# Projections inside the attention's plan, for a hybrid decoder step on one Trainium2 core

## The chip, the cores and the metric

The kernel runs on one core of one Trainium2 chip. The metric is the device time of one execution in microseconds (us); all inputs lie in the device's memory at the start, and the outputs lie there at the end. The names of the engines are those of the profile: PE is TensorE's matrix multiply, PEld its weight load, DVE the vector engine, ACT the scalar engine, POOL GpSimd, and SP the engine that issues nearly all transfers.

## The reference

One inference step of a decoder with two layers, for 256 tokens of a new prompt and 8 decoding sequences with 4 new tokens each (288 tokens in all, width 1024), in float32. Each layer is wrapped by two half-step SwiGLU networks (width 2816). Layer 0 mixes by a short gated convolution, layer 1 by a sparse attention with three branches. The change is in layer 1, whose core is:

```python
q, kv_c, kv_s, kv_w, gates = nsa_project(h, w_in)     # 1024 -> 1024 + 6 * 256 + 48
k_c, v_c = compress(kv_c, ...)                        # one key and value per 32 positions, through gelu
s_c = einsum(q, k_c) * scale ; p_c = softmax(s_c)     # compressed branch
imp = p_c summed over the 4 heads of a group, by blocks of 64
idx = top_k(imp with the first, the current and the previous block forced, 16)
o_s = softmax attention over the 16 chosen blocks     # selected branch
o_w = softmax attention over the last 512 positions   # window branch
o = gates[0] * o_c + gates[1] * o_s + gates[2] * o_w ; y = o @ w_out
```

There are 16 query heads of 64 and 4 key heads. The decoding sequences have 2048 past positions each, in pages of 128 rows that a page table names. The prompt has 8 compressed blocks and 4 selectable ones, so it selects all it may see. The projected keys and values are outputs too.

## The kernel before, in words

All activations stand transposed, features on the 128 partitions and the 288 tokens along the free dimension. A product of float32 numbers is made of three: weights and activations are split into a high and a low part (`whi`, `wlo`, `xh`, `xl`), and hi·hi, hi·lo and lo·hi add up in one bank of PSUM. One output tile of 128 features is thus 8 x 3 = 24 matmuls over 288 columns. `Weights` (from line 171) loads weights in chunks of 1 MB into a ring `raw` of four buffers on SP's queue, and splits them on ACT (`whi`, L238) and DVE (`wlo`, L247) into a ring `split` of four pairs.

The first 800 us hold layer 0 and the first network of layer 1, with the compression of the cached pages spread through them as fill. The function `nsa` (from L828) then has two parts.

- **Projections** (L1032 to L1111), in the order in which they are written: six pairs of tiles for the three kinds of keys and values, one tile of 48 gates, eight tiles of queries `qT`. A helper `later(n, f)` places the small work n ticks behind: the prompt's compression (`cmp_prompt_in`, `cmp_prompt`, 2, 3), the turning of values (`values_in`), the gates (through ACT's sigmoid), and, behind each query tile, that tile's compressed scores (`prompt_cmp`, L1094: the 128 query columns are the stationary operand, 16 compressed keys stream).
- **Attention**, whose order is made by a planner (`Plan`, L127). Each step has an engine, a time that it takes (`TAKES`), what it comes after, buffers that it holds, and a rank. The planner goes through the steps that could start earliest on an engine, within a tolerance `NEAR`, and takes the one of lowest rank; so it writes out an order for each engine, and waits are fitted to it. Ranks are tables of numbers: `HEADS`, `CHUNKS`, `TAILS` for the four pairs of sequences, `UNITS` for the prompt's eight head groups.

For a pair of sequences, a *head* (`small`, `max`, `parts`, `share`, `rank`, `best`) scores the compressed keys and the new tokens, and makes the mask of blocks. Five *chunks* follow (the window and four quarters of the past), each of two pages of 1 MB: scores (`S`, four stationary operands of 32 columns side by side), DVE's masked maximum (`top`), ACT's exponential, four transposes (`turn`), a copy on ACT, and the values (`V`, 16 matmuls). A *tail* weights and sums the five parts, and turns the result into `xh` and `xl` for the output projection (`out` is the matmul with `Sel`). A prompt unit has two sets of scores, eight exponentials, twelve transposes and a value step `p_v`. POOL scales the prompt's exponentials.

TensorE's array is used in several forms, by how many rows and columns the operands take: 128x128 for products and transposes, 128x32 for sequences' scores and values, 128x64 for the prompt's values and compression, 64x128 for the prompt's scores, and a few small ones.

Pages come from `load_pages` (L1012): into four buffers `early`, free `raw` buffers, and, once the products are over, the four `split` pairs. A buffer is refilled after the `V` step that read it. All pages and the weights of the output projection go through SP's one queue, in order. `attention_out` (L1513) multiplies by `w_nsa_out`; its first two tiles go part by part, all hi·hi first. Then the last network and the final norm follow; in the last network, POOL issues eight copies of 1 MB of the window cache from memory to memory (L1554).

Of the kernel before, what the change touches and what calls it, by code (L numbers as in the profile page):

```python
# [50 lines left out]
RINGS = dict(mm=4, tr=2, acc=2, U=2, PA=1, PB=1, S=3, PTs=2, small=2, pc=1, score=1, mk=2, sum=2, PTm=2)  # L51
TAKES = dict(
    small=0.35, max=0.55, parts=0.9, share=0.35, rank=0.25, best=1.2, S=0.9, S2=1.0, top=0.62, top_w=0.8, exp=0.71, turn=0.5, copy=0.49,
    copy_v=0.61, V=1.0, og=0.16, min=0.2, wg=0.38, wg2=1.57, turn_s=0.18, copy_s=0.2, sum=1.36, V_s=0.35, add=0.2, last=0.33,
    own=0.21, out=0.25, oh_s=0.12, ol_s=0.13, cmp=1.38, cmp_e=0.3, cmp_n=1.93, cmp_t=0.33, cmp_c=0.4, s0=1.03, s1=0.65, t0=0.34,
    t1=0.215, e0=0.49, e1=0.385, factor=0.39, f0=1.92, f1=1.0, pturn=0.5, p_v=2.07, oh=0.28, ol=0.34, whi=0.96, wlo=2.4, wlo_v=1.15)
HOP = dict(PE=0.25, ACT=0.16, DVE=0.16, POOL=0.16, DMA=0.1)
LOAD, LAND, LOADED = 2.87, 1.5, 9.6


NEAR = 0.1
CHUNKS = (-56.4, -23.7, -3.8, -22.6, -17.9, 7.3, 5.5, -0.2, 6.9, 9.1, 15.5, 25.2, 19.4, 7.9, 21.5, 16.8, 30.3, 30.7, 32.2, 15.5)
HEADS, TAILS = (-33.5, -10.4, 15.4, 28.6), (-2.5, 14.2, 7.0, -34.2)
UNITS = (-2.6, 4.5, 6.9, 12.9, 16.9, 29.9, 36.5, 29.1)
COMPRESSED = -7.9
# [5 lines left out]
def weight_chunks():  # L71
# [24 lines left out]
    for t in range(6):  # L96
        yield "w_nsa_in", 0, steps[:KD], [range(D + t * 256, D + (t + 1) * 256)]
    yield "w_nsa_in", 0, steps[:KD], [range(D + 6 * 256, N_IN)]
    for pr in range(2):
        for gp in range(2):  # L100
            yield "w_nsa_in", 0, steps[:KD], [range((2 * pr + kp) * 256 + gp * P, (2 * pr + kp) * 256 + (gp + 1) * P) for kp in range(2)]

# [7 lines left out]
class Task:  # L110


    def __init__(self, engine, takes, put, after=(), slots=(), uses=(), rank=0.0):
        self.engine, self.takes, self.put, self.after, self.slots, self.rank = engine, takes, put, after, slots, rank
        self.end = None
        for x in (*slots, *uses):
            x.users.append(self)
# [9 lines left out]
class Plan:  # L127
# [3 lines left out]
    def __init__(self, rings):  # L131
        self.rings = {n: [None] * k for n, k in rings.items()}
        self.free, self.tasks = {}, []
# [6 lines left out]
    def start(self, t):  # L140

        at = self.free.get(t.engine, 0.0)
# [129 lines left out]
def tile_step(ctx, tc, x_turned, vectors, state_turned, cmp_pages, sel_pages, cache_win, win_pages, page_table,  # L272
# [555 lines left out]
    def nsa(at):  # L828
# [260 lines left out]
        def prompt_cmp(u):  # L1089
            if not u:  # L1090
                units["cs"] = accb()
# [522 lines left out]
```

## Time and profile before

| what | us |
|---|---|
| median of 3 runs | 1248.0 (1247.29 to 1249.34) |
| the profiled execution, its own time | 1246.98 |
| its span in the profile | 1245.2 |
| first projection matmul of the attention layer | 811.88 |
| first scores of a chunk of pages | 889.96 |
| first matmul of the output projection | 995.97 |

Times within the profile count from the start of the span. A row of the timeline has its start, its length up to the end of its last instruction, the engine, the line, the operation, and what it writes and reads; matmuls overlap, so a row's length exceeds the distance to the next row's start, and that distance is what a group costs.

### The profile page before, as it was taken

To read this page: it belongs to the slowest core of one execution; us is meant where nothing else is said; L and a number is where in the kernel's file an instruction comes from. 1 tells how busy PE (TensorE), PEld (TensorE's weight loads), DVE (VectorE), ACT (ScalarE), POOL (GpSimd) and SP (SyncE) were. 2 spreads that over 40 slices of the span, in tenths; PEclk is the share of its full clock that TensorE was granted. 3 is DMA by queue.
4 is the path that set the end of the run, shared out by engine and by line. 5 is a ranking of instruction groups with operands and counts; after the bars stand their busy time and mean duration, and the time that the engine had idled before them with its cause. 6 is when DMAs were issued, how large, how long until landed. Compare 5 with 4: busy or idle time off the path is not lost.

```text
span 1245.2 us, 25757 instructions
## 1 busy us (share of the span) xinstructions
PE 1227.8 (99%) x10047; PEld 1162.6 (93%) x10047; DVE 726.3 (58%) x1363; ACT 571.2 (46%) x1011; POOL 241.2 (19%) x237
## 2 busy tenths in 40 slices
PE   9999999999999999999999999999999999999997
PEld 8999999999999999999899999999866699999997
DVE  6663555666765545556564455677568566654554
ACT  6443344533544334335343344544377655433444
POOL 0260121221322201212120012130022222200211
PEclk9999999999999999999999999999999999999999
DMA  7764655756566466546563453496699857565422
GB/s 278 257 216 173 236 171 185 254 186 218 189 213 211 155 206 233 198 151 232 197 237 117 176 174 115 165 339 219 232 362 331 291 209 302 191 249 203 165 101 78
DMA packets 89066, 262.00 MB, mean 210 GB/s; under 512 B 9937, under 2 KB 43090, under 8 KB 73714
## 3 DMA queue, kind: packets, MB, share of 16 engines
q1 hardware_dynamic: 87922, 249.66, 57.0%
q0 software_dynamic: 256, 8.32, 1.7%
q10 hardware_dynamic: 768, 2.38, 0.5%
q8 instruction: 79, 1.29, 0.4%
q14 instruction: 41, 0.34, 0.1%
HBM read 257.31 MB, written 11.35 MB: 216 GB/s over the span
## 4 chain that ended last, share of the span: by engine, by line
PE 91%; DVE 3%; ACT 3%; DMA 2%; issue 1%; SPq 0%; POOL 0%; DVEq 0%; ACTq 0%
PE mm L303 82%; PE tr L303 5%; PE acc L303 3%; PE tr L334 1%; DMA early<-in_sel_pages_dram 1%; DVE wlo L247 1%; ACT S L1211 1%; DMA raw<-in_w_nsa_out_dram 0%; SPq L1008 0%; ACT L534 0%; ACT whi L238 0%; DMA wlo<-in_sel_pages_dram 0%; DMA raw<-in_w_ffa_gu_dram 0%; DVE xT L583 0%; ACT S L1367 0%
## 5 line engine op out<-in xcount | busy, mean ns | idle before, releaser
L303 PE MATMUL mm<-xh,whi 128*128 128x288 f32 x1832 | 543.3, 298 | 3.0 <-DVE xl L1476 1.1
L303 PE MATMUL mm<-xh,wlo 128*128 128x288 f32 x1832 | 539.9, 297 | 0.0
L303 PE MATMUL mm<-xl,whi 128*128 128x288 f32 x1832 | 532.8, 293 | 0.0
L247 DVE TENSOR_TENSOR wlo<-raw,whi 128x1024 fp32r<-128x1024 f32 (+2 forms) x361 | 407.8, 1143 | 94.3 <-ACT whi L238 91.5
L238 ACT ACTIVATE whi<-raw 128x1024 fp32r<-128x1024 f32 (+2 forms) x365 | 343.3, 952 | 100.3 <-PE mm L303 92.9
L303 PEld LDWEIGHTS mm<-xh,whi 128*128 128x128 f32 x1832 | 342.9, 188 | 8.8 <-issue 4.2
L303 PEld LDWEIGHTS mm<-xl,whi 128*128 128x128 f32 x1832 | 346.8, 190 | 0.3
L303 PEld LDWEIGHTS mm<-xh,wlo 128*128 128x128 f32 x1832 | 341.8, 187 | 0.6 <-DVE wlo L247 0.4
L303 PE MATMUL mm<-Ah,wlo 128*128 128x288 f32 x768 | 228.6, 298 | 1.0 <-DVE wlo L247 0.9
L303 PE MATMUL mm<-Ah,whi 128*128 128x288 f32 x768 | 227.9, 297 | 0.0
L303 PE MATMUL mm<-Al,whi 128*128 128x288 f32 x768 | 227.2, 296 | 0.0
L549 POOL TENSOR_TENSOR a<-s,t 128x288 f32<-128x288 f32 x80 | 110.3, 1379 | 517.8 <-DVE t L547 405.5
L303 PEld LDWEIGHTS mm<-Ah,wlo 128*128 128x128 f32 x768 | 144.2, 188 | 2.3 <-DVE wlo L247 2.1
L303 PEld LDWEIGHTS mm<-Ah,whi 128*128 128x128 f32 x768 | 145.0, 189 | 0.6 <-issue 0.4
L303 PEld LDWEIGHTS mm<-Al,whi 128*128 128x128 f32 x768 | 144.6, 188 | 0.0
L552 ACT ACTIVATE Ah<-a 128x288 fp32r<-128x288 f32 x88 | 39.1, 445 | 163.4 <-POOL a L549 150.1
L545 ACT ACTIVATE s<-t 128x288 f32<-128x288 f32 x88 | 39.1, 445 | 156.4 <-DVE t L543 156.3
L547 DVE TENSOR_TENSOR t<-mm,rB 128x288 f32<-128x288 f32 x88 | 40.2, 457 | 115.1 <-PE mm L303 115.1
L583 DVE SCALAR_TENSOR_TENSOR xT<-mm,xT 128x288 f32<-128x288 f32 x64 | 29.2, 456 | 90.1 <-PE mm L303 89.9
L553 DVE TENSOR_TENSOR Al<-a,Ah 128x288 fp32r<-128x288 f32 x88 | 40.8, 463 | 65.9 <-ACT Ah L552 65.9
L303 PE MATMUL tr<-cp,W 128*64 128x256 f32 x512 | 58.8, 382 | 0.0
L387 ACT ACTIVATE xh<-xT,vecT 128x288 fp32r<-128x288 f32 x48 | 25.2, 534 | 62.0 <-DVE xT L583 41.1
(283 smaller groups left out, 847.1 us busy)
## 6 DMA issues: line engine op xcount, KB each, us to landing
raw<-in_w_ffb_gu_dram SPq DMA_DIRECT2D x44, 1024.0 KB, 5.2
raw<-in_w_ffa_gu_dram SPq DMA_DIRECT2D x42, 1024.0 KB, 5.3
cp<-in_cmp_pages_dram SPq DMA_DIRECT2D x256, 128.0 KB, 4.3
early<-in_sel_pages_dram SPq DMA_DIRECT2D x56, 256.0 KB, 5.8
raw<-in_w_ffa_down_dram SPq DMA_DIRECT2D x16, 768.0 KB, 4.5
raw<-in_w_conv_in_dram SPq DMA_DIRECT2D x12, 1024.0 KB, 5.1
raw<-in_w_ffb_down_dram SPq DMA_DIRECT2D x16, 768.0 KB, 5.9
raw<-in_sel_pages_dram SPq DMA_DIRECT2D x48, 256.0 KB, 5.0
```

The costliest lines, as they stand in the source:

```text
L238: self.nc.scalar.activation(parts[0], v, AF.Copy)
L247: (lower or self.nc.vector).tensor_sub(parts[1], v, parts[0])
L303: nc.tensor.matmul(out, lhsT, rhs, start=start, stop=stop, skip_group_check=True)
L334: nc.tensor.transpose(out, in_, ident[:k, :k])
L387: nc.scalar.activation(normed[0][:, d], xT[:, d], AF.Copy, scale=vecT[:, v + d:v + d + 1])
L545: nc.scalar.activation(s1, t1, AF.Silu)
L547: nc.vector.tensor_mul(t2, pu[:, :N], rB)
L549: (nc.vector if last else nc.gpsimd).tensor_mul(a, s1, t2)
L552: nc.scalar.activation(Ah[:, f], a, AF.Copy)
L553: nc.vector.tensor_sub(Al[:, f], a, Ah[:, f])
L583: nc.vector.scalar_tensor_tensor(xT[:, d], py[:, :N], 0.5, xT[:, d], op0=OP.mult, op1=OP.add)
L1211: nc.scalar.activation(o, o, AF.Exp, scale=-1.0, bias=x, accum_out=e)
```

## The change

The queries are projected first, in the written order. Everything else that was projected in the written order, that is thirteen tiles (six pairs and the gates, in the order `SIDES`), becomes steps of the planner (`prod`, with splits `whi` and `wlo_v` and evictions `ev`), and so do the prompt's compression, the turning of values and the gates. So heads and chunks of the sequences, whose compressed keys are there already, may stand between products.

The planner also knows the form of the array: `MODES` gives one to each step of PE, a step in another form than the last one starts `SWITCH` = 0.12 later, and its rank counts `STAY` = 3.71 more. All times and ranks are new, with one rank for a step's first part and another for its second.

The compressed scores of the prompt are one step after the projections: `KcBD`, widened to 32 columns, is now the stationary operand and the queries stream (eight matmuls of 256 columns, four side by side), and a copy on ACT and four transposes bring them into the shape that the rest expects. The sigmoid and the tanh are worked out from ACT's exponential and DVE. The heads leave the scores of the new tokens to a step of their own. The fifth chunk's values are copied out of PSUM like the other four. During the projections weights keep two of the four `raw` buffers and pages get the others; `split` pairs go to pages one by one, as the last products end; one `early` buffer holds the compression weights first. The output projection's first two tiles go by input tile, in the order in which these were finished, hi·hi, hi·lo and lo·hi together. The eight copies of the window cache are issued by ACT.

In the order of the instructions this shows at three places.

PE where the projections end and the attention begins, before (`KcBD` are the prompt's compressed keys, `KcT` those of the sequences, `Qbd` the sequences' queries, `early`, `raw`, `whi` and `wlo` hold pages here, and a product is three rows of `mm<-x..,w..` for each of eight input tiles):

```order
L303 MATMUL mm<-xh,wlo 128x288
L303 MATMUL acc<-KcBD,qT 128x16 x4
L303 MATMUL mm<-early,Qbd 32x512 x4
L303 MATMUL acc<-KcT,Qbd 32x64 x4
L303 MATMUL acc<-kT_9624,Qbd 32x32 x4
L303 MATMUL acc<-kT_9623,Qbd 32x32 x4
L303 MATMUL mm<-early,Qbd 32x512 x4
```

And now, behind the eighth query tile, with thirteen products still to come:

```order
L325 MATMUL mm<-xh,wlo 128x288
L325 MATMUL acc<-KcT,Qbd 32x64 x8
L325 MATMUL mm<-early,Qbd 32x512 x6
L325 MATMUL mm<-raw,Qbd 32x512 x2
L325 MATMUL mm<-xh,whi 128x288
```

The heads of the first two pairs and the scores of two chunks stand ahead of thirteen products. Where the last product (the gates) ends, the new order goes on with the prompt's first unit, the compression (`S_10182` holds its input, `early` its weights), and the values of the first chunk:

```order
L325 MATMUL mm<-xh,wlo 48x288
L356 MATMUL tr<-ident,vT 128x128 x4
L356 MATMUL tr<-ident,vT 32x128 x2
L325 MATMUL mm<-kT_9623,qT 128x256 x2
L325 MATMUL mm<-kT_9624,qT 128x256 x2
L325 MATMUL mm<-kT_9623,qT 128x128 x2
L325 MATMUL mm<-kT_9624,qT 128x128 x2
L325 MATMUL acc<-S_10182,early 64x32 x32
L325 MATMUL mm<-whi,Qbd 32x256 x2
L325 MATMUL mm<-raw,Qbd 32x512 x2
L325 MATMUL mm<-wlo,Qbd 32x256 x2
L325 MATMUL acc<-early,PTs 32x128 x16
```

PE at the end of the attention, before (`Sel` turns the last tail's result for the output projection):

```order
L334 MATMUL tr<-ident,ssm 128x128
L303 MATMUL acc<-raw,PTs 32x128 x16
L303 MATMUL acc<-Vc,sq 32x128 x4
L303 MATMUL acc<-Sel,rms 128x64
L303 MATMUL mm<-xh,whi 128x288 x16
L303 MATMUL mm<-xl,whi 128x288 x16
L303 MATMUL mm<-xh,wlo 128x288 x16
```

And now:

```order
L325 MATMUL acc<-PcT,VcBig 128x256
L325 MATMUL acc<-PA,V_10507 64x256 x2
L325 MATMUL acc<-PB,V_10507 64x128 x2
L325 MATMUL acc<-PA,V_10598 64x256 x2
L325 MATMUL acc<-PB,V_10598 64x128 x2
L325 MATMUL acc<-Sel,rB 128x64
L325 MATMUL mm<-xh,whi 128x288
L325 MATMUL mm<-xl,whi 128x288
L325 MATMUL mm<-xh,wlo 128x288
```

A prompt unit's values stand between the last chunk's values and the `Sel` matmul, and the output projection takes its three parts in turn.

ACT at the same place, before (`whi` are the split weights of the output projection, the last `xh` is the last tail's):

```order
L1376 ACTIVATE PTs<-tr 128x512
L1273 ACTIVATE xh<-acc 128x256
L1441 ACTIVATE sq<-tr 128x128
L238 ACTIVATE whi<-raw 128x1024
L1474 ACTIVATE xh<-acc 128x8x8
L238 ACTIVATE whi<-raw 128x1024 x3
```

And now:

```order
L1604 ACTIVATE sq<-tr 128x128
L260 ACTIVATE whi<-raw 128x1024
L1537 ACTIVATE PTs<-tr 128x512
L260 ACTIVATE whi<-raw 128x1024
L1403 ACTIVATE PA<-tr 128x4x128
L1554 ACTIVATE Og<-acc 128x128
L260 ACTIVATE whi<-raw 128x1024
L1403 ACTIVATE PB<-tr 128x512
L1554 ACTIVATE Og<-acc 128x128
L1422 ACTIVATE xh<-acc 128x256
L1637 ACTIVATE xh<-acc 128x8x8
L260 ACTIVATE whi<-raw 128x1024
```

Three of the four splits have moved ahead of the last tail's result.

The core of the diff, with the tables of ranks left out:

```diff
+MODES = dict(prod="f", turn="f", pturn="f", rank="f", turn_s="f", out="f", cmp_t="f", cs="c", cs_t="f", vt="f", st="f", g2="f", p_v="fp", ch="p",
+             S="c", V="c", small="c", small_n="c", V_s="c", s0="h", s1="h", ch5="q", ch7="r", g4="r")
+SWITCH = 0.12
+NEAR, STAY = 0.07, 3.71
+SIDES = (0, 1, 2, 4, 3, 5)
...
     def start(self, t):
         at = self.free.get(t.engine, 0.0)
+        if t.modes and t.modes[0] != self.mode:
+            at += SWITCH
...
-            at, t = min((x for x in able if x[1].engine == t0.engine and x[0] <= first + NEAR), key=lambda x: x[1].rank)
+            able = [x for x in able if x[1].engine == t0.engine and x[0] <= first + NEAR]
+            at, t = min(able, key=lambda x: x[1].rank + (STAY if x[1].modes and x[1].modes[0] != self.mode else 0.0))
...
         def load_pages():
...
+                room["raw"] = RAW - max(W.live, min(2, W.live + W.stop - W.loaded)) - held["raw"]
...
+        def lower(n, engine, t):
+            W.low(n, engine)
+            load_more(t[-1].end)
+
+        def multiply(n, t, pr):
+            p = units["ps", t, pr] = mmb()
+            hi, lo = W.take()
+            o = p[:hi.shape[2], :N]
+            for k in range(KD):
+                mm(o, hi[:, k], xh[:, k], k == 0, False)
+                mm(o, hi[:, k], xl[:, k], False, False)
+                mm(o, lo[:, k], xh[:, k], False, k == KD - 1)
+            if n >= len(sides) - SPLIT:
+                room["split"] += 1
+                load_more(prods[n].end)
...
+            if n >= ready:
+                high = [step("ACT", "whi", W.high, [wloads[W.units[w][0]], *high], [pairs[n]], rank=r - 7)]
+                got = []
+                got.append(step("DVE", "wlo_v", lambda w=w, got=got: lower(w, nc.vector, got), high, uses=[pairs[n]], rank=r - 6))
+            bank_ = Slot("mm")
+            prods.append(step("PE", "prod", lambda n=n, t=t, pr=pr: multiply(n, t, pr), got[:] + prods[-1:], [bank_], [pairs[n]], r))
...
-        def prompt_cmp(u):
-            if not u:
-                units["cs"] = accb()
-            pv = units["cs"][:, :256].rearrange("p (a u x) -> p a u x", a=2, u=KD)
-            for a in range(2):
-                mm(pv[:, a, u], qT[:, u, a * P:(a + 1) * P], KcBD[:, u // 4], True, True)
+        def prompt_cmp():
+            ps = units["cs"] = accb()
+            for pr in range(2):
+                for g in range(4):
+                    mm(ps[g * 32:(g + 1) * 32, pr * NP:(pr + 1) * NP], KcBD[:, pr], qT[:, pr * 4 + g], True, True)
...
-        for n, (part, x) in enumerate(((0, xh), (0, xl), (1, xh))):
-            for p, u in zip(ps, us):
-                for k in range(KD):
-                    mm(p[:, :N], u[part][:, k], x[:, k], n == 0 and k == 0, n == 2 and k == KD - 1)
+        order = sorted(range(KD), key=lambda u: parts_out[u].end)
+        for k in order:
+            for p, (hi, lo) in zip(ps, us):
+                for part, x in ((hi, xh), (hi, xl), (lo, xh)):
+                    mm(p[:, :N], part[:, k], x[:, k], k == order[0] and part is hi and x is xh, k == order[-1] and part is lo)
...
-            later(1 + 4 * b, lambda b=b: nc.gpsimd.dma_start(win_s[b], cache_win[0, b, NT:]))
+            later(1 + 4 * b, lambda b=b: nc.scalar.dma_start(win_s[b], cache_win[0, b, NT:]))
```

More of the change, by code (lines that the diff above doesn't have):

```diff
@@ L47 @@
 WAITS = (24, 3, 4, 9)
-RINGS = dict(mm=4, tr=2, acc=2, U=2, PA=1, PB=1, S=3, PTs=2, small=2, pc=1, score=1, mk=2, sum=2, PTm=2)
+RINGS = dict(mm=4, tr=2, acc=2, U=2, PA=1, PB=1, S=3, PTs=2, small=2, pc=1, score=1, mk=2, sum=2, PTm=2, vT=2, split=4)
 TAKES = dict(
[L53 to L65, printed above, removed]
+    small=0.15, max=0.37, parts=0.3, small_n=0.15, max_n=0.37, parts_n=0.6, share=0.36, rank=0.21, best=1.38, S=0.87, top=0.61, top_w=0.81,
@@ L940, in nsa @@
[L940 to L949 removed]
+        XP, units = {}, {}
@@ L993, in nsa @@
         room = {"raw": 0, "early": 0, "split": 0}
+        held = {"raw": 0, "early": 0, "split": 0}
         done = []
@@ L1128, in step @@
         def step(engine, name, put, after=(), slots=(), uses=(), rank=0.0):
-            return plan.add(engine, TAKES[name], put, after, slots, uses, rank)
-        loads = [Task("DMA", 0, nothing) for _ in range(len(order) + 2)]
-        queue = [0.0]
+            return plan.add(engine, TAKES[name], put, after, slots, uses, rank, MODES.get(name))
+        loads = [Task("DMA", 0, nothing) for _ in order]
+        wloads = {c: Task("DMA", 0, nothing) for c in range(W.units[W.used][0], W.attention + 2)}
@@ L1139, in load_more @@
                 queue[0] = max(queue[0], at) + LOAD
-                loads[k].end = queue[0] + LAND
+                if x is not None:
+                    x.end = queue[0] + LAND
+            seen[:] = len(pages) + len(done), W.loaded
+        def lower(n, engine, t):
[12 more added lines that the diff above has]
+                load_more(prods[n].end)
@@ new lines, in hidden3, with hidden4 @@
+        def hidden3():
+            x2 = units["hidden"][1]
+            nc.scalar.activation(x2, x2, AF.Exp, scale=-2.0 * (2.0 / math.pi) ** 0.5)
+        def hidden4():
+            x, x2 = units["hidden"]
+            ts(x2, x2, 1.0, None, op0=OP.add)
+            nc.vector.reciprocal(x2, x2)
+            nc.vector.tensor_mul(x2, x2, x)
+        x = Slot("acc")
+        p = step("PE", "ch", cmp_prompt, xps, [x], [xslot], r)
+        units["done"] = [p]
+        p = step("ACT", "ch1", hidden1, [p], uses=[x], rank=r)
@@ L1495, in nsa @@
             prompt_unit(*unit)
-        before = values_of[:PAGES["until"] // 2]
+        before, w = values_of[:PAGES["until"] // 2], W.used + len(sides)
         for n, engine in enumerate(EARLY):
-            before = [step("ACT", "whi", W.high, [*before, loads[len(order) + n // 2]], rank=1000.0 + n)]
-            lower = {"POOL": nc.gpsimd, "DVE": nc.vector}[engine]
-            step(engine, "wlo" if engine == "POOL" else "wlo_v", lambda n=W.done + n, lower=lower: W.low(n, lower), before, rank=1000.5 + n)
-        room["split"] = PAGES["split"]
-        load_more(0.0)
-        for n, x in enumerate(loads[:len(pages)]):
-            x.end = max(0.0, LOAD * (n + 1 - LOADED))
-            queue[0] = x.end - LAND
+            before = [step("ACT", "whi", W.high, [*before, wloads[W.attention + n // 2], last_prod], rank=1000.0 + n)]
+            low = {"POOL": nc.gpsimd, "DVE": nc.vector}[engine]
+            step(engine, "wlo" if engine == "POOL" else "wlo_v", lambda n=w + n, low=low: W.low(n, low), before, rank=1000.5 + n)
         plan.run()
```

425 lines of the change are left out of this document (265 added, 160 removed).

## The prediction

> **What bounds the kernel now.** I read the page first: its engine shares, then the chain of waits.
>
> ```profile
> PE 1227.8 (99%) x10047; PEld 1162.6 (93%) x10047; DVE 726.3 (58%) x1363; ACT 571.2 (46%) x1011; POOL 241.2 (19%) x237
> PE 91%; DVE 3%; ACT 3%; DMA 2%; issue 1%; SPq 0%; POOL 0%; DVEq 0%; ACTq 0%
> ```
>
> PE sets the time nearly everywhere, so a gain must take work from PE or fill its gaps. The change touches the stage from the first projection of the attention layer (811.88) to the first matmul of the output projection (995.97), 184.1 us. The view of busy time by stretches shows where PE is not full there (columns: stretch, its length, busy time and count of PE, PEld, DVE, ACT and POOL, granted clock, DMA share, GB/s).
>
> ```profile
> 811.88:882.00 70.12, 70.12 (x580) 68.16 (x581) 48.01 (x118) 28.61 (x39) 12.19 (x20) 1.00 0.72 251
> 882.00:890.00 8.00, 7.83 (x65) 7.71 (x67) 1.96 (x9) 0.00 (x0) 0.00 (x0) 1.00 1.00 327
> 890.00:915.00 25.00, 21.75 (x354) 14.07 (x354) 21.35 (x109) 18.46 (x69) 2.89 (x2) 1.00 0.85 298
> 915.00:965.00 50.00, 50.00 (x698) 34.05 (x698) 35.78 (x177) 37.35 (x136) 14.46 (x10) 1.00 0.96 348
> 965.00:985.00 20.00, 19.44 (x265) 12.78 (x262) 12.24 (x62) 14.65 (x53) 5.49 (x4) 1.00 0.98 358
> 985.00:995.97 10.97, 8.52 (x124) 5.74 (x122) 5.90 (x25) 6.36 (x17) 0.64 (x2) 1.00 0.50 168
> ```
>
> The projections are full. The attention has 6.4 us of idle PE, nearly all in two places: 3.25 us in its first 25 us, and 2.45 us in its last 11. The clock is 1.00 throughout. From 915 to 985 DMA is all but full too, so a second bound lies close behind PE.
>
> **The change, part by part.**
>
> *Fewer changes of form.* Counted over PE's orders in this stage, matmuls whose form differs from the one before fall from 109 to 84. What one costs, the timeline shows twice:
>
> ```profile
> 937.28 0.64 PE L303 MATMUL acc<-whi,PTs 128*32 128x128 f32 x16
> 937.74 0.62 PE L303 MATMUL acc<-wlo,PTs 128*32 128x128 f32 x16
> 938.29 0.72 PE L303 MATMUL mm<-kT,qT 64*128 64x128 f32 x8
> 939.46 1.04 PE L303 MATMUL mm<-raw,Qbd 128*32 128x512 f32 x8
> 940.32 0.40 PE L303 MATMUL acc<-Vc,sq 128*32 128x128 f32 x8
> 985.97 1.07 PE L303 MATMUL mm<-raw,Qbd 128*32 128x512 f32 x8
> 986.96 1.09 PE L334 MATMUL tr<-ident,S 128*128 128x128 f32 x8
> ```
>
> Sixteen value matmuls take 0.46 up to a group of the same form, and the same sixteen 0.55 up to one of another. Eight scores take 0.86 and 0.99. So a change costs 0.09 to 0.13; 25 fewer are 2.3 to 3.3 us, and I take 2.5, nearer to the first pair, whose two groups follow each other directly.
>
> *Compressed scores.* Groups of four used to stand between query products:
>
> ```profile
> 881.50 0.51 PE L303 MATMUL acc<-KcBD,qT 128*128 128x16 f32 x4
> 881.86 0.38 PE L303 MATMUL mm<-xh,whi 128*128 128x288 f32 x1
> 888.76 0.48 PE L303 MATMUL acc<-KcBD,qT 128*128 128x16 f32 x3
> 889.96 1.07 PE L303 MATMUL mm<-early,Qbd 128*32 128x512 f32 x8
> 929.66 0.61 PE L303 MATMUL mm<-wlo,Qbd 128*32 128x256 f32 x8
> 930.09 1.06 PE L303 MATMUL acc<-early,PTs 128*32 128x128 f32 x32
> 931.08 1.09 PE L334 MATMUL tr<-ident,S 128*128 128x128 f32 x8
> 932.10 1.08 PE L303 MATMUL acc<-raw,PTs 128*32 128x128 f32 x32
> ```
>
> A group costs 0.36, and the last two, with a wait for the last query tile, 1.20: six times 0.36 and 1.20 are 3.4 us. The new step streams 256 columns in the 128x32 form; eight such records take 0.43, and float32 makes sixteen of eight matmuls: 0.86. Four transposes are half of 1.02, 0.5. ACT's copy lies under other steps of PE. Gain 2.0; from 1.6, if the copy delays the transposes, to 2.5, if the scores share a form with their neighbours.
>
> *The front of the attention.* Before, the heads come behind the last query product, and the first chunks wait for them:
>
> ```profile
> 897.32 1.08 PE L303 MATMUL acc<-early,PTs 128*32 128x128 f32 x32 [0.57 <-ACT PTs L1376]
> 899.12 0.64 PE L303 MATMUL mm<-whi,Qbd 128*32 128x256 f32 x8 [0.72 <-DVE nb L1363]
> 914.99 1.05 PE L303 MATMUL mm<-early,Qbd 128*32 128x512 f32 x4 [1.62 <-DMA early<-in_sel_pages_dram]
> 903.20 6.35 DMA early<-in_sel_pages_dram
> 909.57 5.28 DMA early<-in_sel_pages_dram
> ```
>
> The last two rows are the chain of waits: pages requested when the first values freed a buffer. Now the first two heads and two chunks' scores run ahead of thirteen products, so the masks and exponentials of the front lie under some 40 us of products. The two waits of PE before 900, 0.57 and 0.72, I count as gone, 1.3 us (none of it, if the products' own splits hold DVE and ACT, which were busy 48.0 and 28.6 of 70 us there). Of the 1.6 us page wait I count 0.9: two chunks' scores are done earlier, but their buffers are still freed by value steps that follow the products.
>
> *The tail.*
>
> ```profile
> 935.20 0.70 PE L303 MATMUL acc<-PcT,VcBig 128*128 128x256 f32 x2
> 935.83 0.65 PE L303 MATMUL acc<-PA,V 128*64 128x256 f32 x4
> 988.37 1.08 PE L303 MATMUL acc<-raw,PTs 128*32 128x128 f32 x32 [0.31 <-ACT PTs L1376]
> 994.49 1.06 ACT L238 ACTIVATE whi<-raw 128x1024 fp32r<-128x1024 f32 x1 [1.98 <-DMA raw<-in_w_nsa_out_dram]
> 994.50 0.41 PE L303 MATMUL acc<-Sel,rms 128*128 128x64 f32 x2 [1.08 <-DVE rms L1464]
> 995.97 2.41 PE L303 MATMUL mm<-xh,whi 128*128 128x288 f32 x16 [1.06 <-DVE xl L1476]
> ```
>
> A unit's values start in the first row and end at 937.28, where the next group quoted above starts; these 2.1 us now stand ahead of `Sel` and cover its 1.08; with 0.31 that is 1.4. The last 1.06, from `Sel` through ACT and DVE to the first product, has no cover and stays. The weights are no longer late: before they waited for the raw buffer that the value step at 988.37 freed; now three of four splits precede the last result. This is a condition for the new order, because the third matmul already needs a low part. If that cover failed, POOL's split would show:
>
> ```profile
> L247 POOL TENSOR_TENSOR wlo<-raw,whi 128x1024 fp32r<-128x1024 f32 x4 | 9.9, 2467 | 13.4 <-ACT whi L238 13.4
> 847.89 3.18 PE mm L303 x24
> ```
>
> It takes 2.5 us (the second row is for the next part).
>
> *Moved at no cost.* Thirteen products cost 3.2 us each wherever they stand (24 matmuls, 3.18 in the last row, from the chain of waits). Their splits and evictions go with them, on ACT and DVE, which have room in the first row of the stretches. The sigmoid and tanh lose two table loads of ACT, off the path. The window copies leave POOL for ACT in the last network, which this stage does not reach; the same bytes move.
>
> *New waits.* Between the last split pair handed to pages and the first freed buffer, only ten of forty pages have been requested; thirty more go through one queue. I add 0.9 us of waits that the old order did not have (none to 5).
>
> Sum: -2.5 - 2.0 - 1.3 - 0.9 - 1.4 + 0.9 = **-7.2 us**, against the profiled execution's 1246.98: 1239.8. That execution was 1.0 under the median of 1248.0, so the median should be 1240.8. With all costs at their kind ends -3.3 - 2.5 - 1.3 - 1.6 - 2.4 = -11.1; at the others -2.3 - 1.6 + 5 = +1.1.
>
> **The rivals.**
>
> *More than forecast.* Busy PE hides waits: a matmul in flight counts as busy. In the stretch 915 to 965 PE is full by its own row, but its loads only 34.05 of 50. If the new order also closes such hidden gaps, as far as ACT and DVE allow (37.35 and 35.78 of 50), a further 4 us are possible: 1236. For it speaks that the old order ran ACT and DVE chains in this stretch; against it, that 128x32 loads are short and need not fill PEld. [...]
>
> *The vector engines take over.* In part of this stretch ACT never rested:
>
> ```profile
> 950.00:955.00 5.00, 5.00 (x91) 3.42 (x90) 4.01 (x16) 5.00 (x20) 2.89 (x2) 1.00 0.43 159
> 955.00:960.00 5.00, 5.00 (x92) 3.60 (x92) 2.96 (x16) 5.00 (x22) 0.78 (x1) 1.00 0.87 295
> ```
>
> If ACT sets the pace in the attention, saved changes of form only become waits. Left are what lies outside: 2.0 + 1.3 + 1.4 - 0.9, about 4: 1244.
>
> *Pages set the end: slower.* With thirteen products of 3.2, eight of the same, and some 4 us of heads, scores and turns between them, the products end near 811.9 + 67 + 4 = 883. The buffer of the compression weights comes free some 4 us later, at 887. Thirty pages of 1.05 MB follow one another. Behind the last one stand its scores, turns and values and what the new order puts after them, some 12.6 us by the rows above: scores 0.9, two chunks' values 0.9 each, two units' values 2.1 each, 29 transposes at 0.12, 1.2 of small groups, and the wait of 1.06. At 348 GB/s (915 to 965) the pages take 90 us, and the stage ends at 990, 6 us earlier than before; at 298 (890 to 915) 106 us, and it ends at 1005, 9 us later: 1257. It breaks even near 326. Against it: the low rate of that stretch came from a front that freed no buffers. For it: DMA share 0.85 there, and buffers are now freed one by one. As a middle, at 315, it ends 4 us late: 1252.
>
> *The change doesn't do what it says:* changes of form are saved in the planner, but products wait for weights, with two raw buffers instead of four and pages between them in SP's queue. From the split of one chunk to the need of the next but one lie six products, 19 us; two splits (4.6), a landing and two pages ahead of it take about 15:
>
> ```profile
> raw<-in_w_nsa_in_dram SPq DMA_DIRECT2D x10, 1024.0 KB, 5.4
> ```
>
> Four chunks come so late in the order; each 2 us late would cost 8, and nothing would be gained: 1248.
>
> **How the numbers follow.** The forecast (1238 to 1244 by itself) gets 0.50, more than forecast 0.20, the vector engines 0.15, pages 0.09, late weights 0.06. A difference under 0.2%, 2.5 us, can't be told from none. The first three are faster by more than that, save for edges of 0.02: 0.83. Within lie half of the late weights, those edges and a part of the pages at break-even: 0.08. Slower: 0.09. The range from 1233 to 1247 leaves out the slow pages, part of the late weights and the far end of the gain, about 0.15 to 0.2.
>
> **What would show it.** Changes of form: transposes or values of the same count still 0.09 to 0.13 apart by what follows, and no group between query products. Front: no idle time of PE from the end of the products over the next 20 us but for pages. Tail: `Sel` without a wait, about 1.06 in front of the first product, and `whi` ended before it. The whole stage, 184.1 us before, should take 177. The forecast is wrong if PE waits for pages more than 3 us in all, if the products pause for `wlo`, or if PE shows no idle time and the stage is still no shorter than 181.

## The result, and the profile after

The change made the kernel slower: a median of **1254.8 us** (1252.9 to 1258.5, 5 executions) against 1248.0; the ratio is 1.0063 (95% interval 1.0041 to 1.0086). The forecast was 1240.8, with 1233 to 1247 as its range. The profiled execution took 1258.5, the upper end of the five: its trace shows more of the loss than the median has.

The page of the changed kernel, engine shares and the chain of waits:

```profile
PE 1230.6 (98%) x10043; PEld 1165.4 (93%) x10043; DVE 731.3 (58%) x1371; ACT 569.8 (45%) x1012; POOL 234.7 (19%) x227
PE 88%; DVE 6%; ACT 4%; issue 1%; DMA 1%; POOL 0%; SPq 0%; DVEq 0%; ACTq 0%
```

PE is 2.8 us busier than before, in four fewer records, and DVE has doubled its share of the chain. The stage from the first projection to the output projection takes 194.2 us; it was 184.1, and 177 was expected. Busy time by stretches of this stage (columns as before: stretch, length, PE, PEld, DVE, ACT, POOL, granted clock, DMA share, GB/s):

```profile
812.29:838.30 26.01, 26.01 (x194) 25.78 (x194) 21.77 (x59) 10.37 (x12) 3.55 (x9) 1.00 0.94 348
838.30:852.00 13.70, 9.71 (x75) 7.86 (x75) 12.52 (x52) 5.29 (x10) 0.81 (x2) 0.88 0.41 131
852.00:890.00 38.00, 38.00 (x292) 37.76 (x292) 17.43 (x34) 11.99 (x17) 2.63 (x6) 1.00 0.62 219
890.00:920.00 30.00, 27.53 (x418) 19.07 (x417) 17.82 (x83) 16.06 (x57) 4.78 (x3) 0.83 0.95 340
920.00:990.00 70.00, 67.09 (x958) 46.65 (x957) 52.26 (x244) 52.79 (x191) 17.39 (x12) 1.00 0.93 330
990.00:1006.50 16.50, 11.77 (x140) 7.91 (x140) 11.79 (x38) 9.79 (x27) 6.19 (x3) 0.90 0.75 300
sum 194.21, PE 180.12 PEld 145.03 DVE 133.58 ACT 106.28 POOL 35.35; mean PE 30.02 PEld 24.17 DVE 22.26 ACT 17.71 POOL 5.89
```

Two things are new. PE stands idle for 14.1 us (194.2 less 180.1), and it was 6.4 before (184.1 less 177.7). And the clock, 1.00 throughout before, is 0.88, 0.83 and 0.90 in three stretches, the ones in which PE is idle for the largest share (29%, 8% and 29%). The waits of PE in this stage (time in total, times, longest):

```profile
PE mm L325 <- DMA early<-in_win_pages_dram: 2.5, 1, 2.5
PE acc L325 <- DVE PA L1401: 2.4, 1, 2.4
PE tr L356 <- ACT S L1528: 1.7, 3, 1.2
PE tr L325 <- DVE pcs L1467: 1.5, 1, 1.5
PE acc L325 <- DVE Qbd L1087: 1.2, 1, 1.2
PE tr L356 <- POOL S L1381: 1.0, 1, 1.0
```

They lie at three places: the *front* (`Qbd`, `pcs`, the first `S`, 838 to 849), a window *page* at 900, and the *tail* (`S` behind POOL, then `PA`, 996 to 1003).

**The clock.** Cut into windows of 3.413 us, whose edges are those of the clock's steps, the same execution reads:

```profile
844.90:848.31 3.41, 0.93 (x6) 0.56 (x4) 3.00 (x8) 3.31 (x7) 0.00 (x0) 1.00 0.02 5
848.31:851.72 3.41, 3.15 (x14) 3.15 (x15) 3.20 (x13) 1.76 (x4) 0.81 (x2) 0.50 0.51 166
851.72:855.14 3.42, 3.42 (x28) 3.42 (x28) 2.18 (x9) 1.34 (x2) 0.71 (x2) 1.00 0.34 144
899.51:902.92 3.41, 1.24 (x25) 0.78 (x26) 0.00 (x0) 1.51 (x9) 0.00 (x0) 1.00 1.02 380
902.92:906.34 3.42, 3.42 (x36) 2.63 (x39) 2.23 (x11) 1.20 (x5) 0.00 (x0) 0.50 1.02 379
...
909.75:913.16 3.41, 3.41 (x26) 0.99 (x24) 3.07 (x14) 0.60 (x1) 0.16 (x1) 0.50 0.98 331
998.50:1001.91 3.41, 1.29 (x26) 0.62 (x14) 3.13 (x6) 0.55 (x2) 1.73 (x1) 1.00 0.49 151
1001.91:1005.32 3.41, 2.73 (x16) 1.66 (x16) 2.31 (x5) 0.00 (x0) 0.00 (x0) 0.50 0.91 380
```

All the steps of the clock, from 848.3 to the end of the span, are whole multiples of 3.413 us apart. The windows in which PE was busy for 0.93, 1.24 and 1.29 us are followed by a clock of 0.50: for one window after the front and one after the tail, for three (10.2 us) after the page. What half a clock costs, the timeline shows where the first of them ends:

```profile
850.45 0.44 PE L325 MATMUL mm<-xl,whi 128*128 128x288 f32 x1
850.69 0.44 PE L325 MATMUL mm<-xh,wlo 128*128 128x288 f32 x1
...
852.08 0.30 PE L325 MATMUL mm<-xh,whi 128*128 128x288 f32 x1
852.22 0.29 PE L325 MATMUL mm<-xl,whi 128*128 128x288 f32 x1
```

A product's matmul follows the one before it by 0.24 us, and by 0.13 to 0.14 at full clock. Half clock counts as busy (3.42 of 3.42 us in the window from 902.92), so it hides in the engine shares. In the profile before the change the emptiest window ahead of the program's end had 1.79 us busy, and the clock stayed full behind it:

```profile
912.50:915.91 3.41, 1.79 (x8) 0.17 (x4) 2.00 (x10) 1.71 (x8) 0.00 (x0) 1.00 0.98 347
915.91:919.33 3.42, 3.42 (x32) 2.22 (x32) 3.08 (x12) 2.23 (x6) 0.00 (x0) 1.00 1.03 379
```

In none of the three windows ahead of half clock was PE idle throughout, only for more than half of it. The edges lie at other places in each trace: at 912.50 before the change and at 899.51 in the changed kernel, 3.8 windows apart.

### The profile page after: what moved, and what is told of

Read it like the earlier page. It is cut to its first block, busy times and chain, and to the rows that moved or that the text cites. A ratio compares the mean times of both kernels' runs of the same rounds, so it can differ in the third digit from the quotient of the medians.

```text
span 1256.4 us, 25759 instructions
## 1 busy us (share of the span) xinstructions
PE 1230.6 (98%) x10043; PEld 1165.4 (93%) x10043; DVE 731.3 (58%) x1371; ACT 569.8 (45%) x1012; POOL 234.7 (19%) x227
## 3 DMA queue, kind: packets, MB, share of 16 engines
q8 instruction: 79, 1.29, 0.4%
## 4 chain that ended last, share of the span: by engine, by line
PE 88%; DVE 6%; ACT 4%; issue 1%; DMA 1%; POOL 0%; SPq 0%; DVEq 0%; ACTq 0%
PE mm L325 79%; PE tr L325 5%; PE acc L325 3%; DVE wlo L269 2%; PE tr L356 1%; ACT whi L260 1%; ACT S L1360 1%; DMA early<-in_win_pages_dram 1%; DMA xT<-in_x_turned_dram 1%; ACT L556 0%; ACT sq L418 0%; DVE S L1524 0%; ACT PTs L1537 0%; DVE xT L605 0%; DVE xT L1688 0%
```

## The experiments

Four kernels follow from the three places; each leaves the order of all other work as the changed kernel has it. Theory: the new order does save PE's time, but three waits and the half clock behind them cost more. Rival: the new order is itself no shorter, and the waits only show where it isn't.

**1. PE kept busy in the three places.**

```diff
                 t["rank"] = trb()
+                if i == 0:
+                    for _ in range(6):
+                        mm(t["rank"][:, :P], ident, ident, True, True)
...
                     d["pt"] = trb()
+                    if first.pop("turn", 0):
+                        for _ in range(4):
+                            mm(d["pt"][:, :P], ident, ident, True, True)
...
+                            if c == 5 and part == 0 and q == 2:
+                                for _ in range(2):
+                                    for z in (2, 3):
+                                        mm(ps[z * 32:(z + 1) * 32, :256], Qbd[:, 2 * i, z % 2], pages[i, j, 0][0][:, :, :P], True, True)
...
+                if u == 5:
+                    for _ in range(8):
+                        mm(o[:, :P], ident, ident, True, True)
```

> The order is the changed kernel's; in front of the three places where PE stood longest (the first rank of blocks and the first turn of scores, the scores of the second sequence pair's window pages, the values of the last prompt unit) stand 22 more matmuls whose results are overwritten: about 2.1, 0.9 and 1.7 us of PE work, nearly all inside waits of 2.7, 2.5 and 2.4 us. Theory 'half clock' (a window of 3.41 us in which PE was busy for less than half is followed by half clock, for 3.4 us where dense products follow, for 10.2 us where small attention matmuls follow): the three stretches at a clock of 0.50 between 848 and 1006 disappear, the waits stay nearly as long, and the time falls by 3 to 7 us against the changed kernel's 1254.8, to 1248 to 1252. Rival 'the waits alone' (the clock follows the idle time but costs nothing by itself): 1254 to 1257, at most the extra matmuls' own price is added.

Measured: 1252.0 (1250.8 to 1257.8), ratio to the kernel before 1.0042 (1.0026 to 1.0058); the changed kernel had 1.0063. At the front and the tail no half clock was left. The four matmuls at the page were too few, though:

```profile
896.71:900.12 3.41, 1.39 (x26) 0.61 (x18) 0.74 (x8) 1.96 (x9) 0.00 (x0) 1.00 1.04 375
```

1.39 us busy, and four windows at half clock follow, up to 913.8. That was the profiled execution, of 1256.9 us; four of the others, with a mean clock of 0.998, took 1250.8 to 1252.0. One with 0.999 took 1254.5, which the clock doesn't explain; it has no trace. With work that computes nothing the median was 2.8 us lower, but the two intervals overlap, so this alone doesn't show a gain. That half clock has a price of its own, and how large it is, experiments 5, 6 and 9 show better.

**2. The tail's first low part on DVE.** The rows of DVE, POOL and PE in the changed kernel's tail:

```profile
996.30 1.71 DVE L269 TENSOR_TENSOR wlo<-raw,whi 128x1024 fp32r<-128x1024 f32 x1 [2.02 <-ACT whi L260]
996.89 3.34 POOL L269 TENSOR_TENSOR wlo<-raw,whi 128x1024 fp32r<-128x1024 f32 x1
997.94 2.37 DVE L1609 TENSOR_SCALAR rB<-Og,wg 128x128 f32<-128x128 f32 x1
1001.85 0.68 DVE L1401 COPY PA<-tr 128x512 f32<-128x512 f32 x1
1002.59 1.12 PE L325 MATMUL acc<-PA,V 128*64 128x256 f32 x4 [2.38 <-DVE PA L1401]
```

The same operation as in the third row takes 0.28 elsewhere (923.6). Here it ends at 1000.31, 0.08 after POOL's split. The low part of 128x1024 itself took 1.71 beside POOL (1.22 alone) and 3.34 on POOL (2.5 alone).

```diff
-EARLY = ("POOL", "DVE", "DVE")
+EARLY = ("DVE", "DVE", "DVE")
```

> The first early low part of the output projection's weights is computed on DVE, as the two behind it, and no longer on POOL; all else has the same order. Theory 'POOL holds DVE up' (while POOL's 3.34 us split ran, from 996.9 to 1000.2, a DVE operation of 128x128 took 2.37 us instead of 0.28, and the copy to PA came late): no DVE operation in the last 15 us of the attention is longer than 1.3 us, PE's wait for PA falls from 2.38 to under 0.8, and no half clock follows it: 2.5 to 4 us less, 1251 to 1252.5. Rival 'too much work for DVE at the tail': the third split's 1.2 us on DVE delays PA as much as POOL did, and the time stays within 1 us of 1254.8.

Measured: 1255.2 (1252.2 to 1255.6), ratio 1.0056 (1.0043 to 1.0070): no gain in the median, as the rival had it.

```profile
989.96 3.87 POOL L1381 TENSOR_TENSOR S<-S,sm 128x512 f32<-128x512 f32 x2 [7.82 <-PE tr L356]
990.79 4.12 DVE L269 TENSOR_TENSOR wlo<-raw,whi 128x1024 fp32r<-128x1024 f32 x2 [0.59 <-ACT whi L260]
993.89 1.09 PE L356 MATMUL tr<-ident,S 128*128 128x128 f32 x8 [1.97 <-POOL S L1381]
997.39 0.65 PE L325 MATMUL acc<-PA,V 128*64 128x256 f32 x4 [0.27 <-DVE PA L1401]
```

The wait for `PA` went from 2.38 to 0.27, but now DVE's low parts (4.12 for two, 2.4 alone) met POOL's scaling (3.87, 2.89 alone), and PE's wait for `S` grew from 0.98 to 1.97. In both traces operations of POOL and DVE beside each other were stretched, whichever started first (DVE's split at 996.30 in the changed kernel, POOL's scaling at 989.96 here). The tail of this execution, from the transposes of the last unit to the output projection, was still 2.3 us shorter (8.9 us, 11.1 in the changed kernel), without half clock; but it was the fastest of the five. What the slower ones lost, at mean clocks of 0.992 and 0.993, isn't shown. Why the two stretch each other is not shown either.

**3. The late constants out of DVE's way.**

```diff
+        soon = len(todo)
         put(ts, f2, f2, 3, None, op0=OP.bitwise_and)          # token selection, from here on
...
         put(ts, nm, nm, -1.0, -NEG, op0=OP.add, op1=OP.mult)  # masks of the new keys, up to here
+        late = todo[soon:]
+        del todo[soon:]
...
             nc.vector.tensor_mul(dst[:, pr], p[:, :N], rB)    # eviction of a key or value product
+            for f in late[:4]:
+                f()
+            del late[:4]
```

> Of the small constants that DVE builds beside the query products, the 22 that are read only after the products (token selection, masks of the new keys) are built beside the first six evictions of the key and value products; all else has the same order. Theory 'constants in DVE's way' (DVE is busy 34.4 of the 40 us from 812, builds constants from 839.9 to 844.2 and the first heads wait behind them): PE's waits for Qbd, pcs and the first S between 838 and 849 (1.2, 1.5 and 1.2 us) fall to 1.5 together, the half clock behind them goes, and the time falls by 3 to 4.5 us, to 1250.5 to 1252. Rival 'the head chain by itself' (scores, maximum, exponential, share and rank follow each other, with few products to cover them): only the first wait goes, 1 us less.

Measured: 1250.3 (1245.4 to 1254.5, 12 executions), ratio 1.0017 (1.0006 to 1.0028), 4.6 us under the changed kernel. The waits for `pcs` and the first `S` are gone, that for `Qbd` (1.0) stays:

```profile
PE acc L325 <- DVE PA L1407: 2.4, 1, 2.4
PE mm L325 <- DMA early<-in_win_pages_dram: 2.1, 1, 2.1
...
PE acc L325 <- DVE Qbd L1090: 1.0, 1, 1.0
```

So the constants were in the way. The twelve times also go with the clock: 1245.4 at a mean clock of 0.998, 1250.2 at 0.995, 1254.5 at 0.991, one program. A likely reason is that the waits fall differently against the windows of 3.41 us from execution to execution; this is not shown, since only the slowest of the twelve has a trace.

**4. Two stores behind the pages.**

```diff
-            if pr:
+            if pr and t in (3, 5):
+                stores.append((t, dst))        # issued after plan.run()
+            elif pr:
                 nc.sync.dma_start(kv_out[t], dst)
```

> The stores of the last two value tensors, 0.29 MB each, which stood in SP's queue between the pages at 886 and 890, go behind the attention's plan; all else has the same order. Theory 'pages at their rate' (from 880 to 901.6 the queue moved 350 GB/s without a pause, so 0.59 MB are 1.7 us): the window page that PE waited 2.5 us for lands 1.7 us earlier, the wait is 0.8 and PE stays over half busy in that window, so the 10 us at half clock go as well: 4 to 7 us less in executions that had them, 1249 to 1251 in the median. Rival 'the page's own way' (it is asked for at 894.2, when the buffer of the compression weights comes free, and takes 7.4 us whatever lies ahead of it): the wait stays at 2 to 2.5 us and the time at 1254 to 1255.

Measured: 1252.6 (1249.0 to 1254.9), ratio 1.0034 (1.0022 to 1.0046), 2.3 us less, above the 1249 to 1251 that the theory gave. The wait for the page fell from 2.5 to 0.6, about as the queue's rate had it:

```profile
PE mm L325 <- DMA early<-in_win_pages_dram: 0.6, 1, 0.6
```

No half clock follows at 900. In the profiled execution it now followed the tail for three windows: with one cause gone, the others stay.

**5 and 6. The price of a pause by itself,** in the kernel before, where the output projection's products are dense:

```diff
                 p = mmb()
+                if d in (2, 3, 4, 5, 6, 7):     # 6: (3, 6)
+                    nc.vector.tensor_copy(scr[:, 0:1], last_p[:, 0:1])
+                    for _ in range(1):          # 6: range(4), 288 columns
+                        nc.gpsimd.tensor_sub(scr[:, :128], scr[:, :128], scr[:, :128])
+                    mm(p[:, :64], scr[:, :P], scr[:, P:P + 64], True, True)
                 product(p, xh, xl, 0, KD, True, True)
```

> The kernel before, with six pauses of PE put between the products of the output projection: each product from the third on waits, through one extra matmul, for a small operation of POOL behind the product before it, about 1.3 us each by the times of POOL and of the hand-overs, 8 us in all. Between pauses PE works for 3.2 us, so every window of 3.41 us is more than half busy. Both theories: no stretch at a clock of 0.50 in the output projection, and 1247.6 + 8 = 1254 to 1257.

> The kernel before, with two long pauses of PE in place of the six short ones, at the fourth and the seventh product of the output projection, each behind four operations of POOL of 0.8 us: about 4 us each, again 8 us in all. Theory 'half clock': a stretch of 3.4 us at a clock of 0.50 stands behind each pause, in which dense products run at half speed and lose 1.7 us; the time is 2.5 to 4.5 us over the kernel with short pauses, for the same idle time. Rival 'the waits alone': within 1 us of the kernel with short pauses, once both are set against their measured idle time.

Measured: 1279.7 with six pauses (ratio 1.0248), 1266.1 with two (1.0144). Both expectations were wrong on the length: the small copy stood on DVE behind the product's eviction and split, and POOL's sum of squares in front of the small operation (in the second pause the product ended at 1014.6, the copy started at 1016.1, the operation at 1016.8), so the pauses were 2.8 and 6.8 us. In this order six pauses, then two:

```profile
PE mm L303 <- POOL scr L1532: 16.9, 6, 3.2
```

```profile
PE mm L303 <- POOL scr L1532: 13.6, 2, 6.9
```

From the first product to the last matmul the profiled executions take 275.1 and 263.0 us, and 242.6 before: 32.5 and 20.4 more. Not all of that belongs to the pauses. In both traces the window at the attention's end had little work (1.69 and 1.72 us), and half clock followed it at 996.9 and 996.4, ahead of any pause: 3.1 and 3.4 us of matmuls at half speed, worth half of that. Without it, a pause of 2.8 us cost 5.2 ((32.5 - 1.6) / 6), one of 6.8 cost 9.4 ((20.4 - 1.7) / 2): 2.3 and 2.6 on top of the pause. Both have half clock behind their pauses.

**7. A second edit of the tail.** Two early low parts instead of three, on DVE; the first waits for POOL's last scaling, the second for the last copies to `PA`.

```diff
-EARLY = ("POOL", "DVE", "DVE")
+EARLY = ("DVE", "DVE")
...
-            step(engine, ..., before, rank=1000.5 + n)
+            step(engine, "wlo_v", ..., before + (copies if n else scales), rank=1000.5 + n)
```

> Second edit of the tail: only two early low parts, both on DVE, the first not before POOL has scaled the last unit's scores, the second not before the last copy to PA; all else of the changed kernel stays. Theory 'POOL and DVE hold each other up': neither POOL's scaling (2.9 us) nor a DVE operation of the last 15 us is stretched, PE's waits for S and for PA at the tail are under 1.5 us together (3.4 before), no half clock in the tail: 2 to 3.5 us less than 1254.8, 1251.3 to 1252.8. Rival 'the chain itself': the wait moves to S or xl once more, as with all low parts on DVE, and the time stays within 1 us.

Measured: 1251.0 (1247.3 to 1256.0), ratio 1.0026 (1.0010 to 1.0043), 3.9 us less. PE's wait for `PA` is gone; POOL's scaling takes its 2.89 and PE waits 1.0 for it. DVE still isn't free of POOL: three sums beside the scaling take 2.72 instead of 1.20, here and in the next kernel, which has the same tail. But PE no longer waits for them. Half clock is left at the front, for two windows.

**8. Experiments 3, 4 and 7 together.**

> The late constants, the two late stores and this second edit of the tail together, on the changed kernel. Theory 'three waits and the half clock behind them hide the gain': with all three gone hardly an execution shows a clock of 0.50 before the end, the mean clock is 0.997 to 0.998, and the time is 1241.5 to 1244.5, 3 to 6 us under the kernel before: the gain that the new order was forecast to have. Rival 'the order is no shorter': the waits go elsewhere, and the time stays at 1247 to 1250.

Measured: **1244.8** (1243.7 to 1247.7, 11 executions), ratio 0.9979 (0.9969 to 0.9989): faster than both kernels, and just above what the theory gave. It is 10.0 us under the changed kernel; the three edits by themselves gained 4.6, 2.3 and 3.9. The clock is 1.00 in every stretch of the stage:

```profile
811.50:837.50 26.00, 26.00 (x194) 25.77 (x194) 21.80 (x59) 10.36 (x12) 3.54 (x9) 1.00 0.94 348
837.50:851.00 13.50, 12.54 (x111) 11.04 (x111) 11.83 (x43) 7.17 (x13) 1.69 (x4) 1.00 0.51 174
...
885.00:905.00 20.00, 18.81 (x337) 13.44 (x341) 13.98 (x68) 12.72 (x46) 4.79 (x3) 1.00 1.01 363
905.00:975.00 70.00, 66.89 (x967) 46.68 (x971) 54.50 (x254) 54.45 (x198) 17.38 (x12) 1.00 1.00 357
975.00:990.80 15.80, 13.81 (x212) 9.71 (x204) 12.43 (x42) 10.61 (x31) 2.91 (x3) 1.00 0.66 246
sum 179.30, PE 172.04 PEld 140.17 DVE 132.94 ACT 105.78 POOL 31.98; mean PE 28.67 PEld 23.36 DVE 22.16 ACT 17.63 POOL 5.33
```

This is the ledger of the change, since this kernel gives PE the same matmuls in the same order as the changed one (2066 records in this stage). At full clock they keep PE busy for 172.0 us, and the old order for 177.7: the new order saves 5.6. In the changed kernel they took 180.1: 8.1 for half clock, as the halves of the work in its five slow windows also give (1.6 at the front, 5.1 behind the page, 1.4 in the tail). Idle time rose from 6.4 to 14.1: 7.7. Together -5.6 + 8.1 + 7.7 = 10.2, and the stage is longer by 10.1 (194.2 less 184.1). This holds for the profiled execution, the slowest of its five. The median one was 3.7 us faster at a mean clock of 0.994 instead of 0.991; 0.003 of 1255 us is 3.8, so by this estimate it lost about half as much to half clock.

**9. Pauses that leave a window more than half busy.** As experiment 5, with five pauses, and the copy and POOL's operation issued straight behind the product, ahead of its eviction and the sum of squares.

> The kernel before with five pauses between the products of the output projection, now so ordered that POOL has nothing else in front of the small operation: product, hand-over, 0.4 us of POOL, hand-over, about 1.2 us each, 6 us in all. PE works for 3.2 us between them, so no window of 3.41 us is less than half busy. Theory 'half clock from half a window on': no stretch at a clock of 0.50 in the output projection, each pause costs its own length and nothing more: 1247.6 + 6 = 1252.5 to 1255 (the pauses of 2.8 us cost 5.3 us each). Rival 'every pause costs about 2.4 us on top': 5 x 3.6 = 18, 1265.

Measured: 1254.75 (1253.8 to 1255.4), ratio 1.0054 (1.0035 to 1.0074), a clock of 0.998. PE's waits and its emptiest window in this stretch:

```profile
PE mm L303 <- POOL scr L1534: 4.8, 5, 1.6
```

```profile
1005.31:1008.72 3.41, 1.81 (x14) 1.74 (x14) 2.04 (x5) 1.82 (x3) 1.21 (x2) 1.00 0.45 185
```

Five pauses cost 7.3 us, 1.5 each: the 1.0 that PE waited, and half a microsecond that is left for the extra matmul and the hand-over. A window with 1.81 us of work kept the clock, and no half clock followed any pause.

**10 and 11. The price of a change of form,** in the kernel before:

```diff
                             mm(o[q * 32:(q + 1) * 32, :P], ..., s == 0, s == 3)
+                        if s in (0, 2):
+                            mm(o[:32, 256:264], d["PTs"][:, s, :32], vs[0][s][:, 256:264], True, True)   # 11: 64 for 32
```

> The kernel before with 40 tiny extra matmuls (8 columns streamed) inside the 20 value steps, in the 128x32 form of their neighbours, into columns of the bank that nothing reads: 109 changes of form in the stage, as before. Own price 0.03 to 0.1 us each: 1 to 4 us, 1248.6 to 1251.6.

> The same 40 tiny matmuls in the 128x64 form: 189 changes of form, 80 more. Theory 'a change of form costs 0.09 to 0.13 us': 7 to 10.5 us more than with the tiny matmuls of the neighbours' form. Rival 'the 0.1 us belongs to other things at the border of two steps': under 2 us more.

Measured: 1248.6 (ratio 1.0006, 0.9996 to 1.0016) and 1256.5 (1.0069, 1.0046 to 1.0091). The first has 109 changes of form in its trace, the second 189. In the second kernel the tiny matmul covers the rows of two value groups, and the decoding sequences' outputs are not the reference's; the matmuls and their order are as described. The difference of the medians, 7.9 us over 80 changes, is **0.10 us** for one, within what was expected. Busy PE grew by more, 10.3 us (189.9 against 179.6 in the stage), and 2.5 us of idle time went (3.0 against 5.5): a change shows as 0.13 us of busy PE, part of it hidden in waits. One rival is left: in the profile before, the load of a 128x64 operand takes 0.136 us (`PA`), that of a 128x32 one 0.110 (`early` with `PTs`). If none of this were hidden, the 80 wider loads would explain 2.1 of the 7.9 us, and 0.07 would be left for a change.

## Why the prediction was wrong

What the new order was to save came. What failed is the price put on the moved work and the new waits: the first was taken as nothing, the second as 0.9 us, and the clock had no term. By the prediction's terms PE's idle time in the stage was to fall by 2.7 us (-1.3 - 0.9 - 1.4 + 0.9); it rose by 7.7, and half clock added 8.1.

- **Changes of form, -2.5, and compressed scores, -2.0: right.** 0.10 us times 25 is 2.5. The compressed scores take 0.88 us in experiment 8 (0.86 was the estimate), and their four transposes follow without a wait in a group of eight of 1.02:

```profile
899.96 1.07 PE L325 MATMUL acc<-qT,KcBD 128*32 128x256 f32 x16
900.84 1.04 PE L325 MATMUL mm<-early,Qbd 128*32 128x512 f32 x8
```

  Together they were to save 4.5 us of busy PE; 5.6 came. At 0.13 us of busy PE for a change, 25 of them are 3.2 and most of the rest is explained. So of the rival "more than forecast", with 4 us on top, at most 1.1 came, and the 16 us by which the loads fall short of the stretch (34.05 of 50, where the load of a 128x32 operand takes 0.11 us and that of a 128x128 product 0.19) have not turned out to be room that this order could use.
- **"Moved at no cost", and the front, -1.3: wrong, and the step that failed first.** "On ACT and DVE, which have room in the first row of the stretches" was read from a mean over 70 us of the old order. The change puts the query products with their evictions, all the constants and the first heads into the first 40 us. From 812.3 to 852.0 DVE was busy for 34.3 of 39.7 us, and for 17.4 of the next 38.0: the room came only behind the heads. Before, DVE had more room in its first 40 us:

```profile
811.88:852.00 40.12, 40.12 (x351) 38.94 (x352) 28.68 (x74) 16.83 (x26) 10.17 (x18) 1.00 0.92 318
```

  The old front's waits (0.57 and 0.72) went, and `Qbd`, `pcs` and `S` came, 4.0 us, and half clock behind them. Experiment 3 shows that the constants stood behind the last two. And it was their place in DVE's line more than the amount of work: in experiment 8 DVE is as busy (34.5 of the first 40.5 us), but the late constants stand behind what the heads need, and the waits for `pcs` and the first `S` are gone. ACT's table loads did fall, from 15 of 1.28 us in the whole kernel to 13.
- **The page wait, -0.9, and new waits, +0.9 (0 to 5): net nothing was expected.** One wait of 1.6 became one of 2.5. That alone is small; but it left its window 1.24 us of work, and the old wait 1.79. With as much work in that window, 0.55 us more, there would probably have been no 10 us at half clock. Experiment 4 shows the wait's cause, the bytes ahead of it in the queue.
- **The tail, -1.4: wrong.** `Sel` indeed no longer waited, and `whi` ended before it. But POOL's split, held in the prediction to be a price of 2.5 us if it came late, came early and held DVE up (2.37 us instead of 0.28 for a scaling of 128x128); PE's idle time from 990 on is 4.7 us, against 2.45 in the old last stretch. Experiment 7 shows it, and the rows of experiment 2.
- **The clock: not in the sum.** "The clock is 1.00 throughout" was read from the old trace and kept for the new one. The emptiest window ahead of the program's end had 1.79 us of work in that trace, and the fullest one that half clock followed there in any of these traces had 1.72: 0.07 us to spare. One trace was not enough to see this: experiments 5 and 6 have the old order up to the output projection, and in their traces half clock follows an old window of 1.53 us at 911.6 and the windows of 1.69 and 1.72 at the attention's end. So the old order meets half clock too, in some executions. 8.1 us of the profiled execution are this.
- **The products end near 883:** at about 890, with the front's waits and half clock; at about 884 in experiment 8.
- **The rivals.** "Pages set the end" had the right sign and a page wait, but not the mechanism: behind 902 no page is waited for, and experiment 8 moves 357 GB/s from 905 to 975, above the break-even of 326. "The vector engines take over" named ACT's part in the middle; it was DVE, at the front and in the tail. "Late weights" didn't happen: among the waits of the stage none is for a `wlo` of the products.
- **After the stage** a little was lost that was not forecast: 243.2 us from the first product to the last matmul, 242.6 before, with one more wait of 0.6 for a low part, near 1035. In experiment 8 it is 244.1, so that of the 4.8 us that its stage gains 3.3 are left at the end. Why is open.

Of the forecast's -7.2, the kernel of experiment 8 has -4.8 in its stage (179.3 against 184.1); what is missing are the waits that were counted as gone (its stage is idle for 7.3 us, 0.8 more than the old one's). The rival that was missing reads: three waits, each just long enough to cost the clock.

## What to carry to other kernels

The price of a wait on PE depended here on what else its window of 3.41 us held: behind 1.53 us of work or less half clock followed each time, behind 1.79 or more it did not ahead of the program's end. In the changed kernel it cost 1.4, 1.6 and 5.1 us at the three places. So list the windows that are nearly half empty before moving work, and read the clock beside busy time, since half clock counts as busy. Room on an engine is to be read in the stretch where the work will stand, with what stands ahead of it in the engine's line, and not as a mean over the stage where it stood. In the tail here the times that DVE's and POOL's operations take alone didn't hold where the two worked beside each other (2.37 us instead of 0.28 on DVE, 3.34 instead of 2.5 on POOL); nothing on the critical path should have stood behind either there. Which pairs of operations do this was not tried.

## What the runs showed of the hardware

- The half clock, by windows. Of the windows of 3.41 us at full clock that were read in the profiles of these kernels, from 830 us on, every one with 1.53 us of work or less was followed by half clock. Between 1.64 and 1.72 both occurred (1.64 in experiment 7 with half clock, 1.64 in experiment 2 and 1.71 in experiment 5 without). From 1.79 on the clock stayed full, save at the program's end: there five traces have a last window with 1.85 to 2.20 us and half clock behind it. These windows hold matmuls of a single column, whose busy time may count for less; that was not tried. Half a window is 1.71.
- How long it lasts is open. Behind it, dense products got the full clock back after one window where nothing interrupted them (848.31 to 851.72 in the changed kernel), and the attention's small matmuls behind the page after three (902.92 to 913.16) or four (900.12 to 913.77 in experiment 1), though these windows are full by the record (3.41 of 3.41). But in experiment 5 one such window, from 915.0 to 918.4, was enough in the attention too. Whether the form, the weight loads or something else decides was not tried.
- POOL and DVE beside each other: a scaling of 128x128 on DVE took 2.37 us instead of 0.28, a split of 128x1024 took 1.71 instead of 1.22 on DVE and 3.34 instead of 2.5 on POOL, and POOL's scaling of a unit's scores 3.87 instead of 2.89.
- The queue moved 351 GB/s from 880 to 901.6 without a pause, 3.0 us for a page of 1.05 MB; the planner counts 2.8 (`LOAD`), and does not count the stores, the constants, the clock, or POOL against DVE. With three of these put right (experiment 8), the order that is good by its numbers was also faster than the old one on the chip.
